# First MLP: unit 0's weights made on ACT and POOL instead of ACT and DVE, with the operands of four products in borrowed buffers

## The chip, the cores and the metric

One Trainium2 chip; the kernel runs on one of its cores. A core has TensorE (PE, with weight loads shown apart as PEld), VectorE (DVE), ScalarE (ACT), GpSimd (POOL) and SyncE (SP), which here issues all DMAs. The metric is the device time of one execution, in microseconds; lower is better.

## The reference

A trunk of two residual layers over 1024 tokens of width 1024, in float32. Cut to what matters here:

```python
def _conv_ffn(x, w_up, conv_w, conv_b, w_down):      # D_FF = 2816
    g, u = jnp.split(x @ w_up, 2, axis=-1)
    gc = conv_b + sum_j conv_w[j] * shifted(g, j)    # 3 taps, centred, along the tokens
    act = gelu(gc, exact)
    return (act * u) @ w_down

h = x
h = h + pool_mixer(rms_norm(h))        # layer 0: windowed means, then a 256x256 matrix per group
h = h + _conv_ffn(rms_norm(h))         # the first MLP
h = h + diff_attention(rms_norm(h))    # layer 1
h = h + _conv_ffn(rms_norm(h))
out = rms_norm(h)
```

## The kernel before

**Precision.** Every float32 operand of a matmul is split into a high half, rounded by a cast on ACT, and a low half, the difference, made by a subtraction on DVE or POOL. A product is then three matmuls: high by high, high by low, low by high.

**The up-projection by seven products.** `ffn` cuts w_up into 22 units of 128 columns of u and the same 128 columns of g. Each unit is a 2x2 block product: the inner dimension in two halves, the tokens in two halves. It is done with seven block products instead of eight. Their weight operands (`ws[j][i]`, made by `prep(j)`) come from four blocks of the raw weights, u1, u2, g1 and g2: products 1, 2 and 4 take u1, u2 and g2 themselves; with s1 = g1 + g2 and s2 = s1 - u1, product 6 takes s2, product 5 takes s1, product 7 takes u1 - g1, product 3 takes u2 - s2. Their token operands (`ar.x[i]`) are two blocks of the first 512 tokens (1 and 2) and sums with blocks of the second 512 (6, 7, 5, 4, 3). One product is 12 matmuls of 128x512 at L436. `unit(j)` runs products 1, 6, 2, 7, 5, 4, 3, gathers them in the PSUM tiles up_a, up_b and up_c, adds, applies the convolution and gelu, and writes operands of the down-projection to DRAM. `parts` (L393 on ACT, L394 on DVE or POOL) splits one weight operand; L408 makes the sums.

**The token tiles.** Layer 0's mixer ends in `pool_out(tt)` for eight tiles of 128 tokens: `pool_proj` (L862 on PE), the residual add (L175 on DVE, L176 on ACT), the norm (`rstd`, L190 to L197, mostly tiny DVE operations), `xs` (L306 on ACT), transposes (`tp`, L313 on PE), gain (L323 on DVE, L345 on ACT). Tiles 0 to 3 only need a split (L318 on ACT, L319 on POOL). Tiles 4 to 7 need `combine`: sums t, b, xf at L354, L355, L356, L358 on DVE, and five splits whose casts are L318 on ACT and whose subtractions are L319, two on DVE (products 6 and 5) and three on POOL (7, 4 and 3). `each_with_lag` puts a tile's `combine` behind the first part of the next tile.

**Where unit 0's weights stand.** After tiles 0 to 3, with raised priority, `next(mlp)` loads unit 0's raw weights (L388, into two "g" buffers) and makes the operands of products 1 and 2, low halves on POOL. After tiles 4 to 7 in program order come `load(1)` and the rest of `prep(0)`: four sums and five low halves on DVE (`eng` is DVE for unit 0, POOL from unit 1 on). Then `unit(0, prep(1))`, whose steps make unit 1's weights.

**Order of the queues.** Outside `manual_schedule` the order on each engine is made at build time by a list scheduler: it goes by priority, which is program order unless raised, and fills an engine's free time with later work that is ready, by its own cost model. On the chip each engine runs its queue in that order. From unit 1 on the order of PE, DVE and ACT in the MLP is that of the program; POOL's and SP's stay with the scheduler. Tiles of a pool share a fixed number of buffers: "wc" 16 (weight operands, and before that the mixer's weights and tiles 4 to 7's b12 and b22), "s" 4 (sums), "g" 3, "raw" 4, "cm" 1 and "wd" 1. "wd" holds rows of w_down for their combinations (L453 load, L456 to L462 on DVE, L463 store; first used in unit 1), "cm" holds combinations of the gated values (L479, L480; first used in unit 2).

Of the kernel before, what the change touches and what calls it, by code (L numbers as in the profile page):

```python
# [12 lines left out]
F32R = mybir.dt.float32r  # L13
I32 = mybir.dt.int32
AF = mybir.ActivationFunctionType
ALU = mybir.AluOpType
# [4 lines left out]
P = 128  # L21
# [3 lines left out]
NF = DFF // P  # L25
NT = S // P
NK = D // P
ORDER = (0, 4, 1, 5, 2, 6, 3, 7)
PLAN = ("...saq.bS..c.p", "st.aS.m.q.fb....F.c..")
PLAN7 = (".as.b....S.pqc.", "tmsaSqcb..f......F..")  # L30
# [59 lines left out]
def trunk_kernel(  # L90
# [36 lines left out]
    def f32(ap):  # L127
        return ap.bitcast(F32)
# [18 lines left out]

    hnT = [[hp.tile([P, NK, 512], F32R, name=f"hnT_{n}{hf}") for n in ("hi", "lo")] for hf in range(2)]
    h_dram = [[dram.tile([P, D], F32, name=f"h_dram{i}_{t}") for t in range(NT)] for i in range(4)]
# [82 lines left out]

    gcol = cp.tile([P, 4, NK], F32, name="gcol")
    neglam = cp.tile([P, 1], F32, name="neglam")
# [66 lines left out]
    def norm_to_x(layer, tt, ar, h_t, ss):  # L301
# [19 lines left out]
        def gained(q, dst):  # L321
            gk = gcol[:, 2 + layer, 4 * q:4 * q + 4].unsqueeze(2).broadcast_to([P, 4, P])
            V.tensor_tensor(dst, pts[q], gk, ALU.mult)  # L323
            return dst

        q0, q1 = slice(0, 4), slice(4, 8)
        if tt < 4:
            xf = ar.xf[tt] = ar.tile("raw", [P, NK, P], F32, "xf")
            gained(0, xf[:, q0])
# [36 lines left out]
    def each_with_lag(tiles, first, early=None):  # L366
        late = None
        for tt in tiles:
            nxt = first(tt)
            if late is not None:  # L370
                late()
            late = nxt
            if tt == 1 and early is not None:
                early()
        late()

    def ffn(layer, ar, tail, extra=None):
        G = nc.gpsimd
        wup, wdn, cv = w_up[layer], w_down[layer], convp[layer]
        raws, ws = {}, {}  # L380

        def load(j):
            if j >= NF:
                return
            raws.setdefault(j, [])
            for off in (DFF, 0):
                r = ar.tile("g" if layer == j == 0 else "raw", [P, NK, P], F32, "raw")
                nc.sync.dma_start(r, wup[:, off + j * P:off + (j + 1) * P].rearrange("(k p) f -> p k f", p=P))  # L388
                raws[j].append(r)

        def parts(src, eng=G):
            hi, lo = (ar.tile("wc", [P, 4, P], F32R, n) for n in ("w_hi", "w_lo"))
            A.copy(hi, src)  # L393
            eng.tensor_tensor(lo, src, f32(hi), ALU.subtract)  # L394
            return hi, lo

        def prep(j):
            if j >= NF:
                return
            w = ws.setdefault(j, {})  # L400
            ru, rg = raws.pop(j)
            u1, u2, g1, g2 = ru[:, 0:4], ru[:, 4:8], rg[:, 0:4], rg[:, 4:8]

            eng = (V, G)[j > 0]

            def s_tile(a, b, op):
                t = ar.tile("s", [P, 2, 512], F32, "s")[:, 0].rearrange("p (k f) -> p k f", f=P)
                eng.tensor_tensor(t, a, b, op)  # L408
                return t

            w[1] = parts(u1, G)
            if j == 0:
                w[2] = parts(u2, G)
            yield
            s1 = s_tile(g1, g2, ALU.add)
            s2 = s_tile(s1, u1, ALU.subtract)
            w[6] = parts(s2, eng)
            yield
            if j:
                w[2] = parts(u2)  # L420
            yield
            w[7] = parts(s_tile(u1, g1, ALU.subtract), eng)
            yield
            w[5] = parts(s1, eng)
            yield
            w[4] = parts(g2, eng)
            yield
            w[3] = parts(s_tile(u2, s2, ALU.subtract), eng)
            yield
# [293 lines left out]
            return ends[2:]  # L723

        load(0)
        first = prep(0)
        next(first)
        if layer:
            next(first)
        yield  # L730
        load(1)
        for _ in first:
# [17 lines left out]
    ar = Arena("a")  # L750
# [123 lines left out]
    def tail0(tt, r):  # L874
        return norm_to_hnT(ar.h[tt], tt, ar, r)

    mlp = ffn(0, ar, tail0, lambda: before_attention())
    pool_band(0)

# [149 lines left out]
    def proj_qk(j, hf):  # L1029
# [5 lines left out]
        for h in range(2):  # L1035
            acc = ps_pj.tile([P, 512], F32, name="pj")
            n = 0
            for k in range(NK):
                whi, wlo = w_qk[j][k // 2]
                for l, r in ((whi, xhi), (wlo, xhi), (whi, xlo)):  # L1040
                    PE.matmul(acc, l[:, k % 2, h], r[:, k], start=(n == 0), stop=(n == 3 * NK - 1))  # L1041
                    n += 1
# [201 lines left out]
    ar = Arena("b")  # L1244
# [83 lines left out]
    with tc.manual_schedule(engines={mybir.EngineType.PE}):  # L1328
        for g in range(H * NT + 2):
            j, i = divmod(g, NT)  # L1330
# [53 lines left out]
    for j in range(4, 8):  # L1384
        hi, lo = ([ar.tile("wc", [P, 512], F32R, "wo_l") for _ in range(2)] for _ in range(2))
        r = ar.tile("raw", [P, D], F32, "rawo")
        nc.sync.dma_start(r, w_o[0][j * P:(j + 1) * P, :])
        for n in range(2):
            A.mul(hi[n], halves(r)[n], subsc)
            V.scalar_tensor_tensor(lo[n], halves(r)[n], subsc, f32(hi[n]), ALU.mult, ALU.subtract)  # L1390
        grp.append((j, hi, lo))
    mlp = ffn(1, ar, lambda *a: tail1(*a), lambda: final_gain())

    def wo_rest(tt):
# [9 lines left out]

    each_with_lag(ORDER, wo_rest, lambda: next(mlp))

# [55 lines left out]
```

## Time and profile before

| | before |
|---|---|
| three runs, us | 2073.23, 2075.48, 2075.9 (median 2075.48) |
| the profiled execution, us | 2074.96, span 2073.2 |
| mean granted TensorE clock | 0.986 of full speed |
| PE busy | 1999.2 us, 96% |
| DVE busy | 1553.3 us, 75% |
| ACT busy | 1023.5 us, 49% |
| POOL busy | 891.7 us, 43% |

The span runs from the first to the last instruction of the profiled execution; its own time is what the runs are compared in. Busy time is the sum over the span: an engine that is busy 43% of it may still be full in one stage. In the rows of a queue the first number is the start, the second the length, both in us; `out<-in` are the program's names, and the bracket tells how long the engine had stood idle and what released it. A length includes time in which an instruction stands still inside its engine.

### The profile page before, as it was taken

How to read it: one execution, taken by the hardware profiler on the slowest of the kernel's cores; microseconds unless marked ns; L12 is line 12 of the kernel's file. 1: busy time of each engine (PE TensorE's matmuls, PEld its weight loads, DVE VectorE, ACT ScalarE, POOL GpSimd, SP SyncE). 2: the span in 40 equal slices, each digit the busy share in tenths (PEclk: the TensorE clock that was granted, in tenths of full speed). 3: DMA queues.
4: the chain of work that ended last, by engine and by line, in shares of the span. 5: the costliest groups of instructions: out<-in, count | busy, mean ns of one | idle time of the engine just before them, and what ended most of it. 6: DMA issues, size and time to landing. Idle time of an engine off the chain costs nothing.

```text
span 2073.2 us, 27646 instructions
## 1 busy us (share of the span) xinstructions
PE 1999.2 (96%) x9659; PEld 1664.9 (80%) x9659; DVE 1553.3 (75%) x2286; ACT 1023.5 (49%) x1838; POOL 891.7 (43%) x676
## 2 busy tenths in 40 slices
PE   6799999999999999999999998998999999999998
PEld 6678888888888877888888887876888888888886
DVE  7867777777675658999889987767766777775665
ACT  7733333333453646666667666565433333344343
POOL 4499999996000000101110111115999999930000
PEclk9899999999999999999999999998999999999999
DMA  4325464453976522122212115253445445458663
GB/s 172 104 90 174 138 192 143 157 173 128 378 227 209 193 67 67 43 70 65 64 44 75 56 42 188 102 191 114 128 142 192 148 158 175 140 197 334 200 212 133
DMA packets 221720, 301.90 MB, mean 146 GB/s; under 512 B 17852, under 2 KB 142092, under 8 KB 218764
## 3 DMA queue, kind: packets, MB, share of 16 engines
q1 hardware_dynamic: 221580, 300.13, 44.4%
q8 instruction: 76, 1.25, 0.3%
q14 instruction: 64, 0.52, 0.1%
HBM read 196.78 MB, written 90.70 MB: 139 GB/s over the span
## 4 chain that ended last, share of the span: by engine, by line
PE 87%; DVE 6%; ACT 2%; DMA 2%; issue 1%; SPq 1%; DVEq 0%; ACTq 0%
PE dn L610 19%; PE up_b L436 17%; PE up_c L436 11%; PE up_a L436 11%; PE pj L1041 7%; PE sc L1127 5%; PE pj L1083 4%; PE po L1169 3%; PE aT L1158 3%; PE pj L1265 2%; PE pp L862 1%; DVE nm L1129 1%; PE pl L842 1%; PE wo_acc L1265 1%; DMA kf<-t 1%
## 5 line engine op out<-in xcount | busy, mean ns | idle before, releaser
L1109 POOL TENSOR_TENSOR q_lo<-qt,q_hi 128x256 fp32r<-128x256 f32 x64 | 49.6, 776 | 680.5 <-ACT q_hi L1108 626.7
L394 POOL TENSOR_TENSOR w_lo<-s,w_hi 128x512 fp32r<-128x512 f32 x168 | 270.6, 1610 | 19.4 <-ACT w_hi L393 19.1
L610 PE MATMUL dn<-hnT_hi 128*128 128x512 f32 x560 | 218.1, 389 | 0.0
L610 PE MATMUL dn<-hnT_hi,hnT_lo 128*128 128x512 f32 x560 | 217.9, 389 | 0.0
L610 PE MATMUL dn<-hnT_lo,hnT_hi 128*128 128x512 f32 x560 | 217.9, 389 | 0.0
L436 PE MATMUL up_b<-x_hi,w_hi 128*128 128x512 f32 x528 | 207.2, 393 | 5.2 <-ACT x_hi L318 4.4
L436 PE MATMUL up_b<-x_lo,w_hi 128*128 128x512 f32 x528 | 207.2, 392 | 1.7 <-DVE x_lo L319 1.7
L394 POOL TENSOR_TENSOR w_lo<-raw,w_hi 128x512 fp32r<-128x512 f32 x130 | 193.7, 1491 | 30.8 <-ACT w_hi L393 29.6
L436 PE MATMUL up_b<-x_hi,w_lo 128*128 128x512 f32 x528 | 206.5, 391 | 0.0
L393 ACT CAST w_hi<-s 128x512 fp32r<-128x512 f32 x176 | 108.7, 618 | 178.7 <-PE up_b L436 90.0
L1129 DVE TENSOR_REDUCE nm<-sc 128x1 f32<-128x1024 f32 x128 | 155.8, 1217 | 15.1 <-PE sc L1127 14.7
L593 ACT CAST hnT_hi<-mst 128x1024 fp32r<-128x1024 f32 (+1 forms) x76 | 74.7, 983 | 167.2 <-PE dn L610 127.5
L594 DVE TENSOR_TENSOR hnT_lo<-mst,hnT_hi 128x1024 fp32r<-128x1024 f32 (+1 forms) x76 | 86.5, 1138 | 92.0 <-ACT hnT_hi L593 91.9
L1132 ACT ACTIVATE prob<-sc,nm 128x1024 f32<-128x1024 f32 x128 | 142.7, 1115 | 23.8 <-DVE nm L1129 11.4
L436 PE MATMUL up_a<-hnT_hi,w_hi 128*128 128x512 f32 x352 | 138.9, 395 | 5.3 <-ACT g L513 4.7
L436 PE MATMUL up_a<-hnT_lo,w_hi 128*128 128x512 f32 x352 | 138.6, 394 | 0.1
L436 PE MATMUL up_a<-hnT_hi,w_lo 128*128 128x512 f32 x352 | 138.2, 393 | 0.0
L408 POOL TENSOR_TENSOR s<-raw 128x512 f32<-128x512 f32 x84 | 133.2, 1586 | 11.4 <-DMA raw<-in_ffn_w_up_dram 4.1
L436 PE MATMUL up_c<-hnT_hi,w_hi 128*128 128x512 f32 x352 | 137.2, 390 | 0.0
L436 PE MATMUL up_c<-hnT_lo,w_hi 128*128 128x512 f32 x352 | 136.9, 389 | 0.0
L436 PE MATMUL up_c<-hnT_hi,w_lo 128*128 128x512 f32 x352 | 136.9, 389 | 0.0
L393 ACT CAST w_hi<-raw 128x512 fp32r<-128x512 f32 x132 | 81.6, 618 | 84.8 <-PE up_c L436 80.6
(317 smaller groups left out, 5447.6 us busy)
## 6 DMA issues: line engine op xcount, KB each, us to landing
raw<-in_ffn_w_up_dram SPq DMA_DIRECT2D x88, 512.0 KB, 4.4
mst<-m_dram SPq DMA_DIRECT2D x70, 512.0 KB, 5.9
wd<-in_ffn_w_down_dram SPq DMA_DIRECT2D x22, 1024.0 KB, 6.0
wd_dram<-wd SPq DMA_DIRECT2D x22, 1024.0 KB, 6.5
m_dram<-cm SPq DMA_DIRECT2D x80, 256.0 KB, 5.6
wst<-wd_dram SPq DMA_DIRECT2D x40, 512.0 KB, 5.2
m_dram<-gc SPq DMA_DIRECT2D x66, 256.0 KB, 6.4
wst<-in_ffn_w_down_dram SPq DMA_DIRECT2D x30, 512.0 KB, 5.5
```

The source lines that it names most:

```text
L393: A.copy(hi, src)
L394: eng.tensor_tensor(lo, src, f32(hi), ALU.subtract)
L408: eng.tensor_tensor(t, a, b, op)
L436: PE.matmul(acc, l[a][:, k], r[b][:, k], start=first and n == 0, stop=n == 11, skip_group_check=True)
L593: A.copy(h_, x)
L594: V.tensor_tensor(l_, x, f32(h_), ALU.subtract)
L610: PE.matmul(banks[t], l[:, q, cols], r[:, q], start=first and cnt == 0, stop=stop and cnt == 3 * n - 1, skip_group_check=True)
L1041: PE.matmul(acc, l[:, k % 2, h], r[:, k], start=(n == 0), stop=(n == 3 * NK - 1))
L1083: PE.matmul(acc, l[:, k % 4], r[:, k], start=(n == 0), stop=(n == 3 * NK - 1))
L1127: PE.matmul(sc[:, ns_], l[:, c], ks[:, c, ns_], start=(l is qhi), stop=(l is qlo))
L1129: V.tensor_reduce(nm, sc, AX.X, ALU.max, negate=True)
L1132: A.activation(soft[j, i][c], sc, AF.Exp, bias=nm, accum_out=sm[:, c, i:i + 1])
```

## The change

For layer 0 a new generator, `prep_first`, takes the place of `prep(0)`; layer 1 keeps `prep(0)`.

- Products 1 and 2 are made as before, at the same place.
- The rest stands at the same place in the program, but its nine subtractions and additions go to POOL instead of DVE.
- The sums are written over the raw blocks, so no "s" buffers are used: g2 becomes g1 + g2, g1 becomes u1 - g1, u1 becomes s1 - u1, u2 becomes u2 - s2. Product 4's operand is made first, since its block is then overwritten.
- The order is now 4, three sums, 6, 7, 5, one sum, 3; before it was two sums, 6, a sum, 7, 5, 4, a sum, 3.
- The operands of products 7 and 5 lie in the "cm" tile, those of 4 and 3 in the "wd" tile; those of 1, 2 and 6 stay in "wc".

```diff
+AHEAD_OF_UP = (0,)
...
-        def parts(src, eng=G):
-            hi, lo = (ar.tile("wc", [P, 4, P], F32R, n) for n in ("w_hi", "w_lo"))
+        def two_pairs(where):
+            t = ar.tile(where, [P, 2, 2, 4, P], F32R, "w_hl")
+            return [(t[:, i, 0], t[:, i, 1]) for i in range(2)]
+
+        def parts(src, eng=G, into=None):
+            hi, lo = into or [ar.tile("wc", [P, 4, P], F32R, n) for n in ("w_hi", "w_lo")]
             A.copy(hi, src)
             eng.tensor_tensor(lo, src, f32(hi), ALU.subtract)
             return hi, lo
+
+        def prep_first():
+            w = ws.setdefault(0, {})
+            ru, rg = raws.pop(0)
+            u1, u2, g1, g2 = ru[:, 0:4], ru[:, 4:8], rg[:, 0:4], rg[:, 4:8]
+            room = dict(zip((7, 5, 4, 3), two_pairs("cm") + two_pairs("wd")))
+            w[1] = parts(u1)
+            w[2] = parts(u2)
+            yield
+            w[4] = parts(g2, G, room[4])
+            G.tensor_tensor(g2, g1, g2, ALU.add)
+            G.tensor_tensor(g1, u1, g1, ALU.subtract)
+            G.tensor_tensor(u1, g2, u1, ALU.subtract)
+            w[6] = parts(u1)
+            w[7] = parts(g1, G, room[7])
+            w[5] = parts(g2, G, room[5])
+            G.tensor_tensor(u2, u2, u1, ALU.subtract)
+            w[3] = parts(u2, G, room[3])
...
         load(0)
-        first = prep(0)
+        first = prep_first() if layer in AHEAD_OF_UP else prep(0)
         next(first)
         if layer:
-            next(first)
+            next(first, None)
         yield
         load(1)
         for _ in first:
```

## The prediction

> **What bounds the kernel now.** I read the first part of the page, then stretches of time, the waits, and the queues of DVE, POOL and ACT one by one around the first MLP's start.
>
> ```profile
> span 2073.2 us, 27646 instructions
> PE 1999.2 (96%) x9659; PEld 1664.9 (80%) x9659; DVE 1553.3 (75%) x2286; ACT 1023.5 (49%) x1838; POOL 891.7 (43%) x676
> ```
>
> PE is busy 96% of the span, so a change pays only where PE stands still. The stretches below give, in this order, length, PE, PEld, DVE, ACT and POOL busy, granted clock, DMA share and GB/s.
>
> ```profile
> 60.00:70.00 10.00, 10.00 (x87) 10.00 (x86) 6.70 (x18) 5.90 (x14) 3.70 (x3) 1.00 0.14 54
> 70.00:80.00 10.00, 10.00 (x73) 9.05 (x71) 9.45 (x21) 9.41 (x23) 3.64 (x3) 1.00 0.26 105
> ```
> ```profile
> 77.00:84.20 7.20, 3.16 (x16) 2.33 (x14) 7.20 (x14) 5.09 (x13) 5.08 (x3) 1.00 0.41 138
> 84.20:90.00 5.80, 5.50 (x20) 4.15 (x20) 5.34 (x11) 3.81 (x10) 1.29 (x1) 0.71 0.29 92
> 90.00:96.60 6.60, 0.00 (x0) 0.00 (x0) 6.48 (x11) 4.31 (x10) 3.06 (x2) 0.85 0.29 87
> 96.60:108.20 11.60, 3.98 (x12) 2.44 (x12) 10.28 (x13) 6.08 (x14) 7.69 (x5) 0.50 0.17 51
> 108.20:123.50 15.30, 15.29 (x59) 12.30 (x60) 7.97 (x9) 6.34 (x10) 14.44 (x11) 0.89 0.24 69
> 123.50:142.60 19.10, 19.10 (x85) 15.75 (x84) 11.81 (x14) 8.11 (x11) 18.79 (x13) 1.00 0.23 70
> ```
>
> From 77.0 to 108.2 PE works 3.16 + 5.50 + 0 + 3.98 = 12.64 of 31.2 us, so 18.6 us are idle; DVE works 29.3 of them. From 108.2 on PE is full. So the start of the first MLP is set by DVE, and whatever moves the moment 108.2 (call it T) moves the end by the same amount. What PE waits for there, and how long POOL waits (us in total, times, longest; between 66 and 130 us):
>
> ```profile
> PE tp L313 <- ACT xs L306: 6.9, 1, 6.9
> PE up_a L436 <- ACT g L513: 4.1, 1, 4.1
> POOL hnT_lo L319 <- ACT hnT_hi L318: 14.4, 3, 9.9
> POOL x_lo L319 <- ACT x_hi L318: 9.7, 5, 2.8
> ```
>
> Those waits lead back to the combinations of token tiles 4 to 7 on DVE. Its queue (start, length, line, operation, idle before), with unit 0's sums (L408) and low halves (L394) among the tiles' work:
>
> ```profile
> 70.87 0.69 DVE L408 TENSOR_TENSOR s<-raw 128x512 f32<-128x512 f32 x1 [0.41 <-ACT xs L306]
> ...
> 87.35 1.48 DVE L408 TENSOR_TENSOR s<-s,raw 128x512 f32<-128x512 f32 x1
> 89.30 0.69 DVE L323 TENSOR_TENSOR b<-tp,gcol 128x512 f32<-128x512 f32 x1 [0.46 <-PE tp L313]
> 89.90 0.68 DVE L408 TENSOR_TENSOR s<-raw 128x512 f32<-128x512 f32 x1
> ...
> 96.71 0.68 DVE L408 TENSOR_TENSOR s<-raw,s 128x512 f32<-128x512 f32 x1
> 98.62 0.69 DVE L323 TENSOR_TENSOR b<-tp,gcol 128x512 f32<-128x512 f32 x1 [1.23 <-PE tp L313]
> ...
> 99.58 0.68 DVE L354 TENSOR_TENSOR t<-b,b 128x512 f32<-128x512 f32 x1
> 100.17 1.76 DVE L394 TENSOR_TENSOR w_lo<-s,w_hi 128x512 fp32r<-128x512 f32 x1
> 101.86 0.68 DVE L355 TENSOR_TENSOR b<-b,xf 128x512 f32<-128x512 f32 x1
> 102.46 1.75 DVE L394 TENSOR_TENSOR w_lo<-s,w_hi 128x512 fp32r<-128x512 f32 x1
> 104.13 1.74 DVE L356 TENSOR_TENSOR xf<-t,xf 128x512 f32<-128x512 f32 x1
> ...
> 105.95 1.59 DVE L358 TENSOR_TENSOR xf<-xf 128x512 f32<-128x512 f32 x1
> 107.47 0.68 DVE L319 TENSOR_TENSOR x_lo<-xf,x_hi 128x512 fp32r<-128x512 f32 x1
> ```
>
> And POOL's queue:
>
> ```profile
> 61.15 2.55 POOL L394 TENSOR_TENSOR w_lo<-raw,w_hi 128x512 fp32r<-128x512 f32 x2
> 73.61 1.29 POOL L319 TENSOR_TENSOR hnT_lo<-b,hnT_hi 128x512 fp32r<-128x512 f32 x1 [9.91 <-ACT hnT_hi L318]
> ...
> 100.04 1.34 POOL L319 TENSOR_TENSOR hnT_lo<-b,hnT_hi 128x512 fp32r<-128x512 f32 x1 [1.53 <-ACT hnT_hi L318]
> 102.01 1.64 POOL L408 TENSOR_TENSOR s<-raw 128x512 f32<-128x512 f32 x1 [0.63 <-DMA rows<-in_ffn_conv_w_dram]
> 103.62 1.70 POOL L319 TENSOR_TENSOR x_lo<-t,x_hi 128x512 fp32r<-128x512 f32 x1
> 105.29 1.71 POOL L408 TENSOR_TENSOR s<-s,raw 128x512 f32<-128x512 f32 x1
> ```
>
> The reader should see one price twice. A DVE operation on two SBUF tiles takes 0.68 us when POOL is still, and its successor starts 0.59 us later (99.58 to 100.17). While POOL runs, the same shape takes 1.75, and the successor starts 1.69 (100.17 to 101.86) or 1.67 us later. So an overlap with one POOL operation costs DVE 1.68 - 0.59 = 1.09 us. The Trainium skill, "SBUF — State Buffer", section "Who interferes with whom", says that a DVE instruction with two SBUF inputs and a GpSimd instruction that reads SBUF exclude each other for the whole instruction; the rows agree in kind, at 1.09 us each. If instead the loser stood still for a whole POOL operation (1.29 us in the row at 73.61), an overlap would cost 1.29 and the sum below would lose 3 x 0.20 = 0.6 us, an estimate.
>
> **The change, part by part.**
>
> *Nine DVE operations leave: four sums, five low halves.* The sums at 70.87, 87.35 and 96.71 stand ahead of waits (the next tile's L323 waits 0.46 and 1.23 us for PE's transposes after the last two), and the one at 89.90 follows such a wait; I cost them at nothing, at most 0.6 us for that fourth. Three of the low halves come after 108.2, beside a full PE: nothing. The two at 100.17 and 102.46 stand in tile 7's combination, which ends in the x_lo at 107.47 that PE waits for: 1.69 + 1.67 = 3.36 us off the path.
>
> *Nine POOL operations come.* Alone they are 9 x 1.29 = 11.6 us, under overlap 9 x 1.68 = 15.1. POOL stands still for 9.91 us before 73.61, while DVE mostly reads PSUM tiles, and the raw weights are there (unit 0's first low halves run at 61.15). Seven of nine would fit (9.91 / 1.29 = 7.7). They come later in program order than the tiles, but the order is made by filling gaps: DVE's sum at 70.87 came into tile 4's work that way. I take most of them as fitting before 74; the rest fall into POOL's later waits (14.4 + 9.7 - 9.9 = 14.2 us).
>
> *ACT's five high halves are the same casts, earlier.*
>
> ```profile
> 83.59 0.58 ACT L513 COPY g<-up_a 128x512 f32<-128x512 f32 x1
> ...
> 98.78 0.63 ACT L393 CAST w_hi<-s 128x512 fp32r<-128x512 f32 x1
> ```
>
> Product 4's operands no longer wait for a "wc" buffer or a sum, so their cast can go out with the raw tile. ACT is idle 4.1 of 10 us from 60 to 70, but only 0.6 from 70 to 80, where a cast delays a tile by about 0.6. I take 0.3 for one half exposed; bounds 0 (all before 70) and 4 x 0.6 = 2.4. Product 6 alone keeps "wc"; its first cast stood at 98.78, right behind tile 7's scaling, and I leave it there, its low half on POOL by about 102.
>
> *Unit 1's preparation loses its brake.* Unit 0 took 14 "wc" buffers and the four "s" buffers; now it takes six and none. POOL can make unit 1's sums before tile 7 is done, where before it made two (102.01, 105.29). So POOL will be busier beside tile 7. Of tile 7's five two-input operations (L354, L355, L356, L358, L319) two were slowed. Bounds: none slowed, 5 x 0.59 + 0.2 for a small copy = 3.15, x_lo ready at 99.58 + 3.15 = 102.7, gain 108.1 - 102.7 = 5.4; all slowed, 8.4 + 0.2, ready at 108.2, gain 0. I take three, nearest to the rows, since tile 7's own two POOL operations and product 6's low half must run there: 3 x 1.68 + 2 x 0.59 + 0.2 = 6.4, ready at 106.0, gain 2.1.
>
> *The tiles "cm" and "wd" are lent to unit 0.* The first load of wd, issued near the start before, must wait until products 4 and 3 have read it, that is until unit 0 ends.
>
> ```profile
> 123.45 2.72 PE up_a L436 x12
> ```
> ```profile
> wd<-in_ffn_w_down_dram SPq DMA_DIRECT2D x22, 1024.0 KB, 6.0
> ```
> ```profile
> 131.16 1.18 DVE L456 TENSOR_TENSOR wd<-wd 128x512 f32<-128x512 f32 x1
> ```
>
> Unit 1 begins at 123.45; with 0.4 to issue and 6.0 to land the tile is there at 129.9, needed at 131.16: hidden, 1.3 us to spare. If SP issues it late, SP's next weight loads and DVE's queue wait behind it; DVE's additions for products 7 and 5 stand there, and from 2 to 3 us late PE feels it one for one. I take 0, bounds 0 and 2. cm is wanted only in unit 2: nothing. The sums in place hold raw tiles in "g" until POOL's last low half; the third "g" buffer is free for unit 0, so nothing.
>
> Sum: -2.1 + 0.3 = **-1.8 us**. The profiled execution took 2074.96 (span 2073.2), so 2073.2; the median of the runs before is 0.5 higher, so 2073.7. A difference under 0.2% (4.15 us) can't be told from none here.
>
> **Rivals.**
>
> *POOL gives the gain back* (20%). If the weight operations fall among tiles 4 to 6 instead of before 73.6, each that meets the chain costs 1.09. All nine: 9.8, less the idle 0.46 + 1.23 and the removed sums (1.48 + 0.68 + 0.68), 4.5 together, less the 2.1: +3.2. Six of them: 6.5 - 4.5 - 2.1, about 0. For it: POOL's waits there hold 14.2 us. Against it: the earlier gap. 2073.5 to 2078.7.
>
> *The chain on POOL is late: slower* (11%). Product 6's low half now stands behind product 4's and three sums on one slow queue. If product 4's cast on ACT goes out only behind tile 7's casts, POOL has from 100.04 three tile operations and five of unit 0 to do before product 6 is whole: 8 x 1.68, to 113.5, and PE's third matmul of that product needs it: T is 5.3 us late, 2080.8. It decides from the point where that low half ends after 108.2; beyond 0.2%, after 112.3. Against it: ACT had room for L513, of lower priority, at 83.59. The Trainium skill, "GPSIMD Engine Reference", section "Engine selection", advises VectorE for elementwise work, GpSimd being about twice as slow with two inputs; here 1.29 against 0.68, so the trace agrees, and the rule speaks for this rival.
>
> *More is freed* (13%). With POOL quiet beside tile 7 the bound of 5.4 is near, and the sum at 89.90 adds up to 0.6: 4.2 to 6 us, 2069.5 to 2071.3. It needs unit 1's sums to stay late.
>
> *Nothing is moved* (6%): the order of the queues sets T elsewhere, by PE's transposes; within 0.5 us, 2075.5.
>
> **Numbers.** Forecast 50% (its own range 2072 to 2075). Faster is the third rival, 0.13; slower the second, 0.11; the rest 0.76. The range runs from 2069.8, most of the third rival, to 2078.2, nearly all of the first; the second is left out.
>
> **What would show it.** Right: no DVE row at L408 or L394 before unit 1; POOL's wait before tile 4's first hnT_lo shrinks from 9.91 to under 4; tile 7's L354 to L319 take about 6.4 us; PE is full from about 106.4. Wrong: L354 to L358 at 1.7 in tiles 4 to 6; product 6's third matmul waiting for a w_lo of POOL; a DVE wait at L456 on wd's DMA in unit 1; or another length of some stage after 143 us, which no step here expects.

## The result and the profile after

| | before | after |
|---|---|---|
| median, compared on one chip | 2074.44 us | 2079.59 us |
| ratio, 95% interval | | 1.0027, 1.0017 to 1.0036 |
| the profiled execution, its span | 2074.96, 2073.2 | 2079.59, 2077.8 |

The change made the kernel 5.2 us slower in the medians, and the interval lies wholly above 1; the prediction was 1.8 us faster. First the same stretches of time as before, with the same columns.

```profile
60.00:70.00 10.00, 7.82 (x56) 7.02 (x55) 4.24 (x9) 3.93 (x8) 9.77 (x9) 0.96 0.01 2
70.00:80.00 10.00, 9.97 (x75) 9.64 (x74) 6.66 (x20) 8.39 (x20) 5.29 (x5) 0.87 0.26 105
...
96.60:108.20 11.60, 2.76 (x10) 1.94 (x10) 9.00 (x13) 6.90 (x14) 10.24 (x8) 0.50 0.18 51
108.20:123.50 15.30, 13.28 (x42) 9.45 (x43) 6.91 (x6) 3.76 (x7) 15.30 (x12) 0.72 0.28 76
```

Two places differ. From 60 to 70, still inside the mixer, PE was full before and now stands still for 2.2 us, with 56 instructions where there were 87. And from 108.2 to 123.5 it was full and now lacks 2.0 us. POOL works 9.77 of 10 us in the gap, where it worked 3.70: the nine operations did go where the prediction put them.

POOL's and ACT's queues there (start, length, line, operation, idle before and its releaser). Lines of the mixer and the tiles are now higher by one, `parts` casts at L398 and subtracts at L399, lines from `prep` on are higher by 23 (in some experiments by a few more); the sums in place are L411, L412, L413 and L417, unit 1's sums L431.

```profile
63.02 1.28 POOL L399 TENSOR_TENSOR w_hl<-raw,w_hl 128x512 fp32r<-128x512 f32 x1
64.38 1.28 POOL L411 TENSOR_TENSOR raw<-raw 128x512 f32<-128x512 f32 x1
...
69.55 1.27 POOL L417 TENSOR_TENSOR raw<-raw 128x512 f32<-128x512 f32 x1
70.79 2.53 POOL L399 TENSOR_TENSOR w_hl<-raw,w_hl 128x512 fp32r<-128x512 f32 x2
77.75 1.30 POOL L320 TENSOR_TENSOR hnT_lo<-b,hnT_hi 128x512 fp32r<-128x512 f32 x1 [4.44 <-ACT hnT_hi L319]
```
```profile
61.13 0.60 ACT L132 CAST hnT_hi<-pl 128x512 fp32r<-128x512 f32 x1
65.69 0.62 ACT L398 CAST w_hl<-raw 128x512 fp32r<-128x512 f32 x1 [3.97 <-POOL raw L411]
66.22 0.58 ACT L132 CAST hnT_hi<-pl 128x512 fp32r<-128x512 f32 x1
67.04 0.62 ACT L398 CAST w_hl<-raw 128x512 fp32r<-128x512 f32 x1 [0.24 <-POOL raw L412]
67.56 0.58 ACT L132 CAST hnT_hi<-pl 128x512 fp32r<-128x512 f32 x1
70.85 0.62 ACT L398 CAST w_hl<-raw 128x512 fp32r<-128x512 f32 x1 [2.71 <-POOL raw L417]
71.38 0.59 ACT L177 ACTIVATE pp<-ha 128x512 f32<-128x512 f32 x1
```

Here is the first cause. Three casts of summed blocks (products 5, 7 and 3) stand in ACT's queue between the mixer's own splits (L132) and squares (L177). Each waits for a sum on POOL, 3.97, 0.24 and 2.71 us, and what stands behind it waits too: DVE, then PE.

```profile
66.83 0.69 DVE L133 TENSOR_TENSOR hnT_lo<-pl,hnT_hi 128x512 fp32r<-128x512 f32 x1 [3.52 <-ACT hnT_hi L132]
...
72.13 0.15 DVE L191 TENSOR_SCALAR rn_b<-ss 128x1 f32<-128x1 f32 x1 [2.03 <-ACT pp L177]
```
```profile
81.39 0.40 PE L459 MATMUL up_a<-hnT_hi,w_hi 128*128 128x512 f32 x1
```

Unit 0's first product now starts at 81.39; before it stood at

```profile
77.25 0.40 PE L436 MATMUL up_a<-hnT_hi,w_hi 128*128 128x512 f32 x1
```

so 4.14 us are lost before the MLP begins. The execution after had entered the stretch a little earlier, as an operation ahead of the first wait shows, here before and after:

```profile
60.87 0.69 DVE L132 TENSOR_TENSOR hnT_lo<-pl,hnT_hi 128x512 fp32r<-128x512 f32 x1 [0.31 <-ACT hnT_hi L131]
```
```profile
60.23 0.69 DVE L133 TENSOR_TENSOR hnT_lo<-pl,hnT_hi 128x512 fp32r<-128x512 f32 x1 [0.32 <-ACT hnT_hi L132]
```

With these 0.64 us taken off, the loss in the stretch is 4.78 us. The second place is tile 7, DVE and then POOL after the change:

```profile
103.77 0.86 DVE L355 TENSOR_TENSOR t<-b,b 128x512 f32<-128x512 f32 x1
104.67 1.64 DVE L356 TENSOR_TENSOR b<-b,xf 128x512 f32<-128x512 f32 x1
106.34 1.65 DVE L357 TENSOR_TENSOR xf<-t,xf 128x512 f32<-128x512 f32 x1
...
108.07 1.59 DVE L359 TENSOR_TENSOR xf<-xf 128x512 f32<-128x512 f32 x1
109.58 1.76 DVE L320 TENSOR_TENSOR hnT_lo<-b,hnT_hi 128x512 fp32r<-128x512 f32 x1
111.27 1.77 DVE L320 TENSOR_TENSOR x_lo<-xf,x_hi 128x512 fp32r<-128x512 f32 x1
```
```profile
101.48 1.26 POOL L431 TENSOR_TENSOR s<-raw 128x512 f32<-128x512 f32 x1
...
105.72 1.72 POOL L431 TENSOR_TENSOR s<-raw,s 128x512 f32<-128x512 f32 x1
107.39 3.40 POOL L399 TENSOR_TENSOR w_lo<-raw,w_hi 128x512 fp32r<-128x512 f32 x2
```

Both low halves have left the stretch, as predicted. Yet from the first sum, t (L355; L354 before), to the end of product 6's x_lo it takes 113.04 - 103.77 = 9.27 us; before it was 108.15 - 99.58 = 8.57. Unit 1's four sums and two low halves stand beside it without a break: all DVE operations but the first take 1.59 to 1.77, and the low half that PE needs first comes last. So the 3.36 us taken out are put back and 0.7 more.

The balance: 4.78 at the first product, 0.7 in tile 7, 5.5 together. From unit 5 to unit 21, the last of the first MLP, the same operation is 5.22 us late; in unit 21:

```profile
524.76 0.68 DVE L552 TENSOR_TENSOR u<-up_c,u 128x512 f32<-128x512 f32 x1
```
```profile
529.98 0.69 DVE L575 TENSOR_TENSOR u<-up_c,u 128x512 f32<-128x512 f32 x1
```

With the 0.64 of entry taken off this is 5.86, so 0.4 us are not accounted for. This lateness is used below as the trace's own measure ("late at 525"), since spans of single executions also scatter by some microseconds behind it, in the attention: e1's profiled execution is still 2.37 us late at 525 and yet ended at 2073.05 us, under the kernel before, while the median of e1 is 2078.25.

### The profile page after: what moved, and what is told of

It reads as the page before. It is cut to its first block, busy times and chain, and to the rows that moved or that the text cites. A ratio compares the mean times of both kernels' runs of the same rounds, so it can differ in the third digit from the quotient of the medians.

```text
span 2077.8 us, 27636 instructions
## 1 busy us (share of the span) xinstructions
PE 2002.6 (96%) x9659; PEld 1666.4 (80%) x9659; DVE 1548.4 (75%) x2277; ACT 1023.0 (49%) x1838; POOL 900.7 (43%) x685
## 4 chain that ended last, share of the span: by engine, by line
PE 85%; DVE 7%; ACT 3%; DMA 2%; issue 2%; SPq 1%; POOL 1%; DVEq 0%; ACTq 0%; POOLq 0%
PE dn L633 19%; PE up_b L459 17%; PE up_c L459 11%; PE up_a L459 11%; PE pj L1064 7%; PE sc L1150 5%; PE pj L1106 4%; PE po L1192 3%; PE aT L1181 3%; PE pj L1288 2%; DVE nm L1152 1%; PE wo_acc L1288 1%; DMA kf<-t 1%; PE pp L885 1%; ACT prob L1155 1%
## 5 line engine op out<-in xcount | busy, mean ns | idle before, releaser
L399 POOL TENSOR_TENSOR w_lo<-s,w_hi 128x512 fp32r<-128x512 f32 x168 | 268.1, 1596 | 19.7 <-ACT w_hi L398 19.3
L399 POOL TENSOR_TENSOR w_lo<-raw,w_hi 128x512 fp32r<-128x512 f32 x131 | 193.4, 1478 | 37.3 <-ACT w_hi L398 37.3
L398 ACT CAST w_hi<-s 128x512 fp32r<-128x512 f32 x172 | 106.1, 618 | 172.8 <-PE up_b L459 82.5
L431 POOL TENSOR_TENSOR s<-raw 128x512 f32<-128x512 f32 x84 | 133.3, 1587 | 10.2 <-DMA raw<-in_ffn_w_up_dram 4.2
L398 ACT CAST w_hi<-raw 128x512 fp32r<-128x512 f32 x132 | 81.5, 618 | 83.9 <-PE up_c L459 81.8
```

## The experiments

Theory Q: ACT's in-order queue, the casts that wait for POOL. Theory C: what POOL does beside the token tiles costs their operations on DVE. The rivals were D (these overlaps cost nothing, something else is slow) and two of the prediction: the chain on POOL is late, and the wait of "wd" for unit 0. The versions below e3 in the table were made when e1, e6, e5 and e3 had shown neither theory alone to be enough. The "before" beside each is that of its own comparison; "entry" is how much later than in the kernel before the operation shown at 60.87 starts, "x ready" the end of product 6's last x_lo, and "net of entry" the lateness at 525 less the entry.

| version | median (before) | ratio, 95% | entry | first product | x ready | late at 525 | net of entry |
|---|---|---|---|---|---|---|---|
| after | 2079.59 (2074.44) | 1.0017 to 1.0036 | -0.64 | 81.39 | 113.04 | +5.22 | +5.86 |
| e1, casts on POOL | 2078.25 (2074.47) | 1.0001 to 1.0020 | -0.50 | 76.74 | 110.47 | +2.37 | +2.87 |
| e6, unit 1's sums held | 2078.17 (2074.47) | 1.0006 to 1.0024 | +0.20 | 82.26 | 113.13 | +4.65 | +4.45 |
| e5, both | 2074.83 (2074.47) | 0.9993 to 1.0011 | -0.03 | 77.21 | 109.51 | +1.04 | +1.07 |
| e3, sums, low halves on DVE | 2079.53 (2074.47) | 1.0009 to 1.0027 | -0.35 | 76.49 | 113.37 | +5.77 | +6.12 |
| e7, e3 and sums held | 2075.50 (2072.81) | 1.0009 to 1.0033 | -0.28 | 76.55 | 107.94 | +1.22 | +1.50 |
| e8, before, sums held | 2072.55 (2072.81) | 0.9989 to 1.0007 | +0.56 | 77.79 | 106.75 | -1.14 | -1.70 |
| e9, e5, product 3 held | 2078.87 (2072.81) | 1.0019 to 1.0042 | +0.50 | 77.73 | 108.10 | +3.52 | +3.02 |
| e2, no lent buffers | 2081.74 (2072.81) | 1.0029 to 1.0053 | +0.09 | 77.31 | 108.90 | +7.86 | +7.77 |
| e10, 6 and 7 early, holds | 2075.00 (2074.71) | 0.9996 to 1.0014 | -1.52 | 75.71 | 107.66 | -0.09 | +1.43 |
| e11, the same, no holds | 2077.60 (2074.71) | 1.0003 to 1.0021 | +0.07 | 77.31 | 112.47 | +4.92 | +4.85 |
| e12, only 6 early, holds | 2070.57 (2074.45) | 0.9977 to 0.9995 | -0.49 | 76.75 | 104.76 | -2.40 | -1.91 |

Each version's trace is one execution, and the entry is its scatter: e6 differs from the changed kernel only in what stands behind unit 0's preparation in the program, and yet they enter 0.84 us apart. So times of different executions are compared net of it where it matters. Net of entry the first product comes between 76.8 and 77.3 in every version but the changed kernel and e6, where it comes at 82.0 and 82.1. The expectations call tile 5's operation at L355 a square; it is the first sum, t, of its `combine`.

**e1: the three waiting casts on POOL itself.**

```diff
-            A.copy(hi, src)
+            (cast or A.copy)(hi, src)
...
-            w[7] = parts(g1, G, room[7])
+            w[7] = parts(g1, G, room[7], G.tensor_copy)     # and so for 5 and 3
```

> As the changed kernel, but the high halves of products 7, 5 and 3 are cast on POOL instead of ACT, so that no cast that waits for a sum of POOL stands in ACT's queue; nearly every other instruction keeps its place. Theory Q (the 5 us are lost because these casts stand in ACT's queue ahead of the mixer's last splits and of the first squares, and wait there for POOL's sums): unit 0's first product starts at 77 us instead of 81.4, tile 7 ends (last x_lo) about 4 us earlier, near 109 instead of 113.0, and the time falls by about 4, from 2079.6 to about 2075.5. Rival P (POOL is what is late: it has nine operations more before tile 4): POOL now has twelve more, its operations for tile 4 start later still, and the time stays at 2079.6 or rises. Rival D (the loss lies behind unit 0: wd's late load, or another order there): no change of the time.

The first product is back at 76.74, PE full up to there: Q is right as to the place. But only 2.85 of 5.22 us come back at 525 (2.99 of 5.86 net), and less in the medians, 1.3 us. The rest is what the expectation's rival P names, a longer row on POOL, as POOL's and DVE's queues show:

```profile
74.41 1.80 POOL L399 TENSOR_TENSOR w_hl<-raw,w_hl 128x512 fp32r<-128x512 f32 x1
76.17 1.75 POOL L320 TENSOR_TENSOR hnT_lo<-b,hnT_hi 128x512 fp32r<-128x512 f32 x1
77.88 1.74 POOL L320 TENSOR_TENSOR x_lo<-t,x_hi 128x512 fp32r<-128x512 f32 x1
79.59 1.71 POOL L320 TENSOR_TENSOR x_lo<-xf,x_hi 128x512 fp32r<-128x512 f32 x1
```
```profile
78.39 1.78 DVE L320 TENSOR_TENSOR x_lo<-xf,x_hi 128x512 fp32r<-128x512 f32 x1
...
80.22 1.62 DVE L320 TENSOR_TENSOR hnT_lo<-b,hnT_hi 128x512 fp32r<-128x512 f32 x1
81.76 1.74 DVE L355 TENSOR_TENSOR t<-b,b 128x512 f32<-128x512 f32 x1
```

The weight work ends at 76.2, not before 73.6; tile 4's three splits on POOL, due at 73.6, queue behind it in an unbroken row, and beside that row tile 4's last operations on DVE take 1.78 and 1.62 where 0.68 is the free length. Tile 5's first sum starts at 81.76; before, 79.60. In the changed kernel itself this did not show: POOL's weight work ended at 73.32, and ACT's wait had moved the tiles 4 us away. Most of this crowding is e1's own, though: the three casts that it brings take 0.61 + 0.61 + 0.96 = 2.18 us on POOL. Without them, and without the wait on ACT, POOL would have been about 0.35 us late for tile 4 (73.96 net of entry against 73.61), an estimate.

**e6: unit 1's sums held until tile 7's first high half**, by four one-column copies that take the "s" buffers first; **e5** has both edits.

```diff
             w[3] = parts(u2, G, room[3])
+            for _ in range(4):
+                d = ar.tile("s", [P, 2, 512], F32, "gate")
+                G.tensor_copy(d[:, 0, 0:1], f32(ar.x[6][0])[:, 0, 511:512])
```

> As the changed kernel, but four tiny copies on POOL hold the four buffers of unit 1's sums until tile 7's token operand of product 6 is cast, so that POOL makes these sums behind tile 7 instead of beside it. Theory Q leaves the first 4.1 us as they are (first product at 81.4). Theory C (the gain at tile 7 was eaten because unit 1's sums on POOL slowed its DVE operations): the stretch from tile 7's t to its last x_lo, 9.3 us in the changed kernel, falls to about 6 to 6.5, and the time falls by about 3, to 2076.6. If the length of this stretch does not hang on POOL, it stays at 9.3 and the time at 2079.6.

> Both edits together: casts of products 7, 5 and 3 on POOL, and unit 1's sums held until tile 7 is nearly done. If Q and C are both right and independent, the gains add: first product at 77, tile 7's stretch 6 to 6.5 us, last x_lo near 106, time about 2072.5, that is some 2 us under the kernel before (2074.4). If only Q is right, 2075.5; if only C, 2076.6; rival P: no better than the changed kernel.

In e6 the stretch of tile 7 fell from 9.27 to 7.4 us (105.77 to 113.13), less than C expected, as two low halves still run beside it. Part of this gain was eaten ahead of it: the ten matmuls ahead of tile 6's transposes took 4.43 us (89.26 to 93.69) where they had taken 3.43 (88.38 to 91.81), at a granted clock of 0.50 against 0.68, and DVE waited 2.99 us for these transposes instead of 1.88. That the first product came at 82.26 is entry (82.06 net of it, 82.03 in the changed kernel). In e5 the time of the kernel before is reached, not the 2072.5 that were expected: +1.04 at 525, and tile 5's first sum still at 82.23. Net of entry e1 gives back 3.0 us, e6 1.4 and both 4.8, so the two roughly add.

**e3: the same nine operations on DVE, in the lent buffers; e7: e3 with unit 1's sums held.**

```diff
-            w[4] = parts(g2, G, room[4])
-            G.tensor_tensor(g2, g1, g2, ALU.add)
+            w[4] = parts(g2, V, room[4])
+            V.tensor_tensor(g2, g1, g2, ALU.add)     # and so for the rest
```

> The engine alone undone: sums in place and lent buffers as in the changed kernel, but the nine additions and subtractions on DVE. Theory Q: the same casts now wait for DVE's sums, which take 0.7 us instead of 1.3 and run in DVE's free time between the mixer's splits, so the mixer's last splits come less than 1 us late, the first product starts by 78, and most of the loss goes: about 2074 to 2076. Only product 6's low half stays beside tile 7. If the loss came from the lent buffers or the sums in place (rival D), it stays: 2079.6.

> The version with sums and low halves on DVE in buffers lent, and unit 1's sums on POOL held until tile 7's first high half. Without the hold unit 0's first product came at 76.5 and yet unit 1 was 5.6 us late, with unit 1's sums on POOL from 94.7 on and tile 6's and 7's two-input operations on DVE at 1.6 to 1.75 us. Theory C: held, those run alone, unit 1 comes 3 to 4 us earlier, 2075.5 to 2076.5. Rival (DVE's own extra work is the cost): little change, 2078.5 to 2079.5.

e3's first product comes on time, which fits Q: on DVE the sums are quick. But the time did not come back, so Q isn't all of it: unit 1's sums, freed by the sums in place, now run on POOL from 94.73, beside tiles 6 and 7, and with them held (e7) 4.55 of the 5.77 us are back at 525 (4.6 net of entry), somewhat more than the 3 to 4 expected, in a stretch of tile 7 that falls from 11.77 to 7.19 us. That is the clearest price of C.

**e8: the kernel before with nothing but the hold.**

> The kernel before, with nothing moved, and four tiny POOL copies of tile 7's first high half (each into one of the four "s" buffers) after unit 0's preparation, so that unit 1's sums on POOL come only behind tile 7's splits. Theory C (a POOL operation beside a DVE operation of a token tile costs the tile about 1.09 us): the two sums that ran at 102.01 and 105.29 beside tile 7 go, two overlaps fewer, T about 2 us earlier, 2072.4 against 2074.5 of the kernel before in its last comparison. Rival (POOL's sums beside tile 7 fill time in which the tile waits for ACT anyhow): no change, 2074.5. If unit 1's weights become late instead, PE waits in unit 1 and it is 1 to 3 us slower.

```profile
104.10 0.68 DVE L394 TENSOR_TENSOR w_lo<-s,w_hi 128x512 fp32r<-128x512 f32 x1
104.70 0.68 DVE L356 TENSOR_TENSOR xf<-t,xf 128x512 f32<-128x512 f32 x1
```

The operations that took 1.75 and 1.74 are at 0.68; x is ready 106.75 - 100.15 = 6.60 us after the start of the first sum, which was 8.57, so 2.0 us as C expected. At 525 1.14 are left (1.70 net of entry), and the medians (0.9989 to 1.0007) can't tell it from no change.

**e9: e5 with product 3's cast and low half also held behind tile 7**, by a one-column copy into its first buffer.

```diff
+            G.tensor_copy(room[3][0][:, 0, 0:1], f32(ar.x[6][0])[:, 0, 511:512])
             w[3] = parts(u2, G, room[3], G.tensor_copy)
```

> The version with the casts of products 7, 5 and 3 on POOL and unit 1's sums held until tile 7, and product 3's cast and low half held there too, so that POOL is free about 2.5 us earlier, before tile 4's first low half is due (73.6). Theory C: in the version without this, POOL's 74.9 to 83.4 was one unbroken row and tile 4's and 5's operations on DVE beside it took 1.2 to 1.8 us in place of 0.68, so tile 5's square came 2.2 us late; with POOL free at 73.4 tile 5's square (L355) is back at about 79.6 to 80 (it was 82.2), unit 1 begins 1 us before its place in the kernel before, not 1 us behind it: about 2073. Rival (tile 5 is late for another reason, such as PE's transposes or ACT): L355 of tile 5 stays at 82 and the time at 2074.8. If product 3's operands come too late, PE waits for them at the end of unit 0: 1 to 3 us slower.

```profile
80.74 1.75 DVE L355 TENSOR_TENSOR t<-b,b 128x512 f32<-128x512 f32 x1
```
```profile
134.73 1.77 DVE L483 TENSOR_TENSOR wd<-wd 128x512 f32<-128x512 f32 x1 [4.55 <-DMA wd<-in_ffn_w_down_dram]
```
```profile
112.07 16.10 SPq L389 DMA_DIRECT2D raw<-in_ffn_w_up_dram  x3
128.26 0.53 SPq L480 DMA_DIRECT2D wd<-in_ffn_w_down_dram  x1
```
```profile
138.82 0.50 PE L463 MATMUL up_b<-x_hi,w_hi 128*128 128x512 f32 x1 [2.86 <-DVE g L558]
```

The first half of the expectation held: tile 5's first sum is back at 80.74, and unit 1's first additions came 1 us ahead of before. Then a third cost appeared, which the prediction had named and priced as covered: "wd" is lent, so its load stands late in SP's queue, behind three raw loads that wait for POOL (16.10 us). It lands for 134.73, DVE waits 4.55 us, PE 2.86. The expectation had looked for a late operand at the end of unit 0; it is a late load in unit 1.

This cost belongs to e9 and not to the loan alone. In e5 the same tiles are lent, x is ready only 1.4 us later than in the kernel before (109.51 against 108.15), and DVE does not wait:

```profile
124.31 0.37 SPq L479 DMA_DIRECT2D wd<-in_ffn_w_down_dram  x1
```
```profile
132.19 1.17 DVE L482 TENSOR_TENSOR wd<-wd 128x512 f32<-128x512 f32 x1
```

There the last raw load ahead of it went out at 122.92, behind a low half on POOL that started at 121.58. In e9 POOL comes to that low half only at 126.48, the raw load follows at 127.80, and wd's load at 128.26. In the changed kernel (128.17, used at 136.58) and in e7 (123.47, 132.60) there is no wait either.

**e2: no lent buffers**, all operands in "wc", sums in place and low halves on POOL.

> The changed kernel with one part undone: no lent buffers, all operands of unit 0 in "wc" as before, sums in place and low halves still on POOL. Theory Q (casts in ACT's queue that wait for POOL's sums hold the mixer's last splits): the casts find no "wc" buffer early, so they come at tile 7, the first product of unit 0 is back from 81.4 to about 77.3; but the low halves then run on POOL beside tile 7 and end late, which is the prediction's own slower rival: PE waits for POOL's low halves after 108, 2078 to 2081. If the lent buffers themselves were what costs (the wait of wd's load for unit 0), the time goes back to 2074.5.

```profile
PE up_b L458 <- ACT w_hi L398: 11.3, 1, 11.3
...
PE up_b L458 <- POOL w_lo L399: 0.7, 1, 0.7
```

Wait of PE in us, times, longest, 100 to 120 us. This is the prediction's own slower rival: the first product is back (77.31), the chain on POOL comes at tile 7 and PE waits for product 6 until 113.16. So the lent buffers are needed for early work. That the loan of "wd" makes no engine wait is seen in e5 and e7 rather than here, where the early work is gone with the loan.

**e10, e11, e12: versions meant to avoid all three costs.** e10 makes only products 6 and 7 early, on POOL with their casts, in "cm"; "wd" isn't lent; 5, 4 and 3 stay on ACT and DVE, held behind tile 7 by a one-column ACT copy into their first buffer; unit 1's sums are held. e11 is e10 without the holds. e12 makes only product 6 early, from sums that need no "s" buffer, and holds unit 1's sums as e6 does (cut; the lines taken out are not shown):

```diff
+            room6, _ = two_pairs("cm")
+            G.tensor_tensor(g1, g1, g2, ALU.add)
+            G.tensor_tensor(u1, g1, u1, ALU.subtract)
+            w[6] = parts(u1, G, room6, G.tensor_copy)
             G.tensor_tensor(u2, u2, u1, ALU.subtract)
+            d7 = ar.tile("s", [P, 2, 512], F32, "s")[:, 0].rearrange("p (k f) -> p k f", f=P)
+            V.tensor_tensor(d7, g2, u1, ALU.subtract)
+            x6 = f32(ar.x[6][0])[:, 0, 511:512]
+            for i, src in ((7, d7), (5, g1), (4, g2), (3, u2)):
+                pair = [ar.tile("wc", [P, 4, P], F32R, n) for n in ("w_hi", "w_lo")]
+                A.copy(pair[0][:, 0, 0:1], x6)
+                w[i] = parts(src, V, pair)
...
```

> Only the two products whose low halves stood inside tile 7's combination (6 and 7) are made early on POOL, casts too, in the two pairs of "cm"; "wd" isn't lent; products 5, 4 and 3 keep "wc" and DVE, but a one-column ACT copy of tile 7's high half into each of their first buffers holds them behind tile 7; unit 1's sums are held by four tiny POOL copies. Theory (three causes: ACT's casts that wait for POOL's sums, POOL beside the tiles on DVE, the wait of wd's load for unit 0): none of them is left, so unit 0's first product stays at about 77, tile 7 loses 3.4 us of low halves and one or two overlaps, and has only POOL's own two splits beside it: T about 105 to 106 in place of 108.2, 2 to 3 us faster than the kernel before (2070.5 against 2072.8 to 2074.5). Rival (the start of the MLP is set by PE's transposes and ACT once DVE is relieved): T moves under 1 us and the time stays within 1 us of before.

> The same without any hold: products 5, 4 and 3 and unit 1's sums come when their data and buffers allow. Theory: ACT casts them in tile 7, two low halves of DVE and unit 1's four sums on POOL fall beside tile 7 again, so its stretch from L355 to the last x_lo is back at 8.5 to 9.3 us and the time at that of the kernel before or up to 1 us above it. Rival (the holds do nothing): the same time as with them.

> Only product 6 is made early, on POOL with its cast, in one pair of "cm", from sums in place that need no "s" buffer (g1+g2, then minus u1; product 7's operand is g2 minus that, on DVE): POOL has six operations, about 7 us, in its idle 9.9 us before tile 4. Products 7, 5, 4 and 3 keep "wc", ACT's casts and DVE, held behind tile 7 by one-column ACT copies; unit 1's sums are held too; "wd" isn't lent. Theory (the three causes): unit 0's first product at about 77, tile 5's square (L355) at about 79.6 as before, tile 7's stretch from L355 to the last x_lo about 5.8 us in place of 8.6, unit 1 begins 2.5 to 3 us earlier than in the kernel before, time 0.10 to 0.15% under it. Rival (with DVE relieved the start is set elsewhere, by PE's transposes behind unit 0's products or by ACT): tile 7 starts later by what the stretch loses, and the time is that of the kernel before within 1 us.

e10 missed. Its one "s" buffer is not free before the mixer's end, so POOL lost the gap:

```profile
69.38 1.28 POOL L411 TENSOR_TENSOR s<-raw 128x512 f32<-128x512 f32 x1 [7.21 <-ACT xs L307]
```

and its weight work fell beside tiles 4 and 5 as in e1; tile 7's stretch was 5.84 us as expected, and both together gave nothing. e11 differs from it by the holds alone and is 5.01 us later at 525, but only 3.4 net of entry, since e10 entered 1.52 us early, and 2.6 in the medians. Its stretch of 8.92 us came as expected; without the holds not only unit 1's sums but also two low halves on DVE stand in it, so this is not a price of C alone. e12 has both, the early work in POOL's gap and the short tile 7:

```profile
60.67 1.29 POOL L399 TENSOR_TENSOR w_lo<-raw,w_hi 128x512 fp32r<-128x512 f32 x1
...
67.61 1.30 POOL L399 TENSOR_TENSOR w_hl<-raw,w_hl 128x512 fp32r<-128x512 f32 x1
73.12 1.30 POOL L320 TENSOR_TENSOR hnT_lo<-b,hnT_hi 128x512 fp32r<-128x512 f32 x1 [4.21 <-ACT hnT_hi L319]
```
```profile
98.92 0.68 DVE L355 TENSOR_TENSOR t<-b,b 128x512 f32<-128x512 f32 x1
99.64 1.64 DVE L356 TENSOR_TENSOR b<-b,xf 128x512 f32<-128x512 f32 x1
...
104.08 0.68 DVE L320 TENSOR_TENSOR x_lo<-xf,x_hi 128x512 fp32r<-128x512 f32 x1
```

POOL is done at 68.9 with 4.21 us to spare, the tiles run as in the kernel before, tile 7 takes 104.76 - 98.92 = 5.84 us, and the first MLP is 2.40 us earlier at 525, 1.91 net of entry. The median is 2070.57 against 2074.45, ratio 0.9986, 0.9977 to 0.9995, as expected. The interval lies wholly below 1; but 0.14% is less than the 0.2% that the prediction held for the least that can be told here, and it is one comparison of the best of twelve versions. Of the 3.9 us in the medians the trace shows 1.9 in the first MLP; where the rest is from was not settled, and 1.9 lies inside the interval too. How much of it the early product 6 brings is open: the hold alone (e8) is 1.70 us earlier net of entry.

## Why the prediction was wrong

The time came out 1.4 us above the range and on the other side of the kernel before. In the prediction's sum -2.1 + 0.3 both terms failed: the first came out at +0.7, the second at 4.8. Step by step:

- *What bounds the start.* Right: DVE's tiles set T, and what moves T moves the end. e12 is that sentence used, though not in full: net of entry x is 2.9 us earlier, and 1.9 of it is kept at 525.
- *Nine POOL operations come, most before 74.* Right, and more so than said: all nine. The prediction stopped there.
- *"ACT's five high halves are the same casts, earlier": the step that failed.* It priced a cast by its length, 0.63, and looked for room for it on ACT; the sum got 0.3, its upper bound was 2.4. A cast of a sum starts when the sum ends, and the first of these sums stood fourth in an unbroken row on POOL, each at about 1.27 us. The measured cost is 4.14 us at the first product, 4.78 net of entry. It is shown by e1, which takes the casts out of ACT's queue, by e3, which makes their sums quick, and by e2, where they come later: each gets the first product back to about 77. The prediction asked what is queued behind a wait for SP and for POOL, not here. The Trainium skill, "PSUM — Partial Sum Buffer", section "Engine vs sequencer instructions", says that ScalarE's queue is strictly first in, first out; the rows at 65.69 and 66.22 agree: a mixer split that needs nothing from POOL starts only behind the cast.
- *Tile 7 with three of five operations slowed: mis-sized.* 6.4 us were forecast, 9.27 measured. Four of the five were slowed (its bound for all five was 8.6), and the order of the two low halves on DVE, which changed places, adds another 1.69 us. "Unit 1's preparation loses its brake" named the mechanism rightly; e3 against e7 prices it at 4.6 us, where the sum allowed 3 x 1.09 = 3.3; there the sums also slow tile 6.
- *The lent "wd": hidden, 1.3 us to spare.* Right. In the changed kernel its load is issued at 128.17 and used at 136.58 without a wait; with 0.4 to issue and 6.0 to land that leaves 2.0 us, an estimate. It does not hang on the other losses, since e5 and e7 show no wait either. The condition that the prediction named, "if SP issues it late", is what e9 brought about: 4.55 us on DVE.
- *The rivals.* "POOL gives the gain back" described what e1 shows (tile 5's first sum 2.2 us late), though there most of it comes from e1's own casts; its ceiling of +3.2 was too low because it did not count ACT. "The chain on POOL is late" is e2, 8.9 us in the medians. Neither is what decided.

## What to carry to other kernels

When an operation moves to a slower engine, follow its consumers too: a short operation that now waits for it holds everything behind it in its own queue, so cost the move by the producer's end and not by the consumer's length. Work that is moved out of a stretch frees buffers, and what was waiting for those buffers comes into the stretch; a hold (a tiny write that depends on the event behind which the work shall stand) was worth about as much as the move: 1.70 us for e8 against 1.91 for e12, net of entry. Undo suspected causes together as well as singly, and count what the remedy itself adds: e1's casts crowded POOL, and e9's order made a load late. Before two traces are compared by a moment, compare them at a moment ahead of the change.

## What was not expected of the hardware

- A cast of 128x512 on POOL costs no more than on ACT, 0.61 us in e12 and e5 against 0.62 on ACT in the changed kernel, where the two-input operations on POOL take 1.27 to 1.30. Beside a DVE that works in SBUF it took up to 0.96 (73.84 in e5).
- An overlap lengthens the operations of both engines: on DVE from 0.68 us to between 1.59 and 1.77, on POOL from 1.28 to 1.71 or so. The Trainium skill, "SBUF — State Buffer", section "SBUF: two separate sides", says that of a DVE operation with two SBUF inputs and a GpSimd operation that reads SBUF, whichever starts first has their shared pair of ports for the whole instruction, and the other fully blocks. The rows agree in kind, not in length: in tile 7 of the changed kernel the operations of each engine start about 1.68 us apart, less than 0.68 + 1.29 = 1.97, and less than the 0.59 + 1.24 = 1.83 at which operations follow each other without an overlap (on DVE 99.58 to 100.17 before, on POOL 68.31 to 69.55 after).
- In the mixer PE lost more than its idle time. From 60 to 77 us it stood still for 2.21 of 17 us after the change, but did 104 instead of 144 instructions, at a granted clock of 0.90; before it was 1.00. Taken by single us, the clock after the change is 1.00 up to 69, 0.55, 0.50, 0.50 and 0.74 in the four us from 69 to 73, and 1.00 again from 73. In these four us PE is busy without a break and does 27 instructions, where it does 10 to 12 in each us from 60 to 65. They come right behind the waits for ACT: from 65 to 69 PE was busy for 1.82 of 4 us, with no single idle time above 1.49. So a part of what the first cause costs is paid at the lower clock, behind the waits.

```profile
60.00:77.00 17.00, 17.00 (x144) 16.73 (x143) 13.15 (x31) 12.31 (x29) 6.42 (x5) 1.00 0.17 66
```
```profile
60.00:77.00 17.00, 14.79 (x104) 13.78 (x103) 7.89 (x24) 9.83 (x24) 13.08 (x11) 0.90 0.16 63
```
